# Weights split ahead at a closer pace, and attention's visits, early output tiles and item distance in another order, in a hybrid encoder step

## Chip, cores and metric

One core of a Trainium2 chip. The metric is the device time of one execution in microseconds (us); the time before is the median of 3 runs. PE is the matrix engine (PEld its weight loads), DVE, ACT and POOL are the vector, scalar and GpSimd engines, SP issues nearly all DMAs.

## Reference

A trunk of two layers over 1024 prompt frames and 32 sample frames, computed as one set of 1056 columns. Layer 0 has an mLSTM mixer, layer 1 a windowed attention with a sink per head and ALiBi; both have a SwiGLU FFN and a LayerNorm after each part.

```python
kv = (x @ w_kv).reshape(B, T, 2, N_KV_HEADS, HEAD_DIM)      # layer 1: two K/V heads, 64 wide
q = (x @ w_q).reshape(B, nc, CHUNK, N_KV_HEADS, GROUP, HEAD_DIM)     # 16 query heads, chunks of 64
s = jnp.einsum('bcqhgd,bckhd->bchgqk', q, k).astype(F32) * (HEAD_DIM ** -0.5) + bias
mx = jnp.maximum(jnp.max(s, -1, keepdims=True), sk)
p = jnp.exp(s - mx)
p = p / (jnp.sum(p, -1, keepdims=True) + jnp.exp(sk - mx))
mix = jnp.einsum('bchgqk,bckhd->bcqhgd', p.astype(v.dtype), v).reshape(B, T, D_ATT) @ w_out
x = layer_norm(DEEPNORM_ALPHA * x + mix, ln_g[layer, 0], ln_b[layer, 0])
x = layer_norm(DEEPNORM_ALPHA * x + swiglu(x, w_gu[layer], w_down[layer]), ln_g[layer, 1], ln_b[layer, 1])
```

## The kernel before

Activations lie transposed, model dimension on partitions: `act` (f32) and `sx`, its high and low half in fp32r. Every product of f32 values is three matmuls (L433 to L435): weight high by activation high, weight high by activation low, weight low by activation high. So each weight is split too: ACT casts the high half (L258, `wh`), and POOL or DVE subtracts (L260, `wl`). The class `Weights` walks a list of units (weight tiles of 128 x 1024) in the order in which PE will want them. It loads each raw (L172, `wr`, four buffers), splits it half by half into five slots, and takes the next as a slot falls free and 1.7 planned us have passed (`FEED_W`). Units in `W.ready` are not split there: their halves were stored in DRAM (`halves`) and are only loaded (L253).

**Order.** All engines run their instructions in the order in which the program emits them, and there is one emitting program. It emits dense matmuls (`gemm`), and after each k step it tells a `Weave` how long the three matmuls should take: 3 x (max(columns, 256) / 2400 + 0.003) planned us. The Weave then steps its side tasks, generators that emit a few instructions and yield a pause in planned us. So a pause says how much dense work is emitted until the task's next piece, not a time on the chip.

**`split_before`** is such a task. It starts in the first up tile of layer 0's FFN (in `summed`) and stores the halves of the 18 weights in `BEFORE` (wkv 0 and 1, wqb 0 to 7, wout_b 0 to 7): load `wraw` (L1318), pause; then for each half a cast on ACT into the one buffer `whi` (L1322), a pause of 1.5, a subtraction on DVE in place (L1324), a pause of 1.8, two stores (L1327), and a pause. There is one `wraw` and one `whi`, so the next cast waits for the store of the last. It is drained at the latest at the end of the down projection.

**The FFN** has, in each layer, 20 up tiles (`up_tile`) of seven products each, by a scheme of seven products for eight, with banks `A` and `B`; ACT copies bank A between products. Then come four down blocks of two tiles (`down`, here called down tiles, the seven products again), whose banks DVE adds into act (L1587, L1589). From the last up tile on, X is reloaded from DRAM (L1535) for the down tiles. Layer 1's FFN runs the same code without `split_before`.

**Attention** covers the 16 heads as 8 pairs j, two to a `jp`, and the columns as 9 blocks b of 128 (the ninth is the sample), three to a group g (384, 384 and 288 columns). A visit is one (jp, g): two query projections (`q_group`, 48 matmuls of the group's width) and six items (j, b). `JG` lists the visits: first (0,0) to (3,0), then for each jp group 1 and group 2. An item passes through scores (L1879, bank `psS`), exponential on ACT (L1900), scaling on POOL (L1913), transposes (L1938, bank `T`), halves (L1942, L1943), for each second item the values (L1967, one bank `O`) and `place`, which adds the result into act (L1981, L1985). The task `attention` runs these stages as a pipeline; `GAP_A` is its pause after a score and after a transpose, and twice that after values, 3 x GAP_A per item. The main loop emits the query projections of the next visit and first waits, emitting nothing dense, until the last visit but one has been scored.

**Output projection.** `out_tile` (L1270 adds its bank into act) multiplies one output tile of 128 rows with one quarter of 264 columns. The first three tiles of quarter 0 (`EARLY`) are emitted inside attention, in the visits (0,2), (1,2) and (2,2); the first of them drains attention until group 0 is placed, and the splitting of group 0. `mixed_parts` is a task that splits the placed attention output into sx (cast on ACT L463, low half L464) and reloads the residual into act (L1244, L1246, `scrx`). Quarter 0 reads `U_OUT_B[0]`, from stored halves; quarters 1 to 3 read `U_OUT_B[1]`, the same weights split again: the first two with POOL, the others with DVE.

Of the kernel before, what the change touches and what calls it, by code (L numbers as in the profile page):

```python
# [31 lines left out]
EARLY = 3  # L32
# [13 lines left out]
RAW = 4  # L46
SLOTS = 5
GAP_M = (0.6, 1.666, 1.519, 1.5)
GAP_A = 0.46

FEED_W = 1.7

# [18 lines left out]
CH = [(c, c * P, P if c < 8 else DEC, c // 3, (c % 3) * P) for c in range(9)]  # L71
# [233 lines left out]
def kernel(ctx: ExitStack, tc: tile.TileContext, A, O):  # L305
    nc = tc.nc
    ctx.enter_context(tc.manual_schedule())
    wv = Weave()
# [34 lines left out]
    for j in range(PAIRS):  # L343
        U_Q.append(add("wqk", 2 * j))
        U_K.append(add("wqk", 2 * j + 1))
        v = ("wv", 2 * j - 2) if j else ("wvg", 0)
# [21 lines left out]
    U_KV, U_QB, U_OUT_B = [], [[], []], [[], []]  # L368
# [2 lines left out]
        U_QB[0] += [add("wqb", u) for u in range(b, b + 4)]  # L371
    for jp in range(QH // 4):
        U_QB[1] += [add("wqb", 2 * jp + i) for i in range(2)]
        if jp < EARLY:
            U_OUT_B[0].append(add("wout_b", jp))
    U_OUT_B[0] += [add("wout_b", u) for u in range(EARLY, 8)]
    U_OUT_B[1] += [add("wout_b", u) for u in range(8)]
    add_ffn(1)
# [2 lines left out]
    on_vector.update((u, f) for u in U_Q[:1] for f in range(2))  # L381
    W = Weights(nc, base, units, pairs, on_vector, set())
    BEFORE = [("wkv", i) for i in range(2)] + [("wqb", i) for i in range(8)] + [("wout_b", i) for i in range(8)]
    for us in (*U_KV, *U_QB, U_OUT_B[0]):
        name = "wkv" if len(us) == 2 else "wqb" if us is not U_OUT_B[0] else "wout_b"
        W.ready.update((u, BEFORE.index((name, i))) for i, u in enumerate(us))
    W.early = {up[i] for up in U_UP for i in range(FIRST, FT)}
    wv.feed = W.feed

# [48 lines left out]
    def psbank():  # L438
        return new(psx[1][0], "d", [P, 512], F32, bufs=psx[1][1])
# [9 lines left out]
    def wcols(u):  # L449
        a, b = W.get(u)  # L450
        return tiles_of(a) + tiles_of(b)
# [10 lines left out]
    def split_act(k, g, low=nc.vector):  # L462
        nc.scalar.copy(sxh[k][g][:], act[k][g][:])  # L463
        low.tensor_sub(sxl[k][g][:], act[k][g][:], sxh[k][g][:].bitcast(F32))  # L464


    def group(g):
        return slice(g * N4, (g + 1) * N4)


    QUARTERS = [(group(g), (g % 2, slice(0, N4))) for g in range(4)]
# [606 lines left out]
    task = gtask = None  # L1078
# [153 lines left out]
    def mixed_parts(src, free, mixed, pauses, low=(nc.vector,), runs=WHOLE):  # L1232


        for (g, ks), pause in zip(runs, pauses):
            t0, n = GRP[g]
            while not free(g):
                yield 0.3
            for k in ks:
                while not mixed(k, g):  # L1240
                    yield 0.3
                split_act(k, g, low[k % len(low)])
                if g == 0:
                    nc.sync.dma_start(act[k][g], src[:, k, t0 : t0 + n])  # L1244
                elif k % 4 == 3:
                    nc.sync.dma_start(act_g[g][:, k - 3 : k + 1], src[:, k - 3 : k + 1, t0 : t0 + n])  # L1246
                yield pause
            if ks[-1] == KT - 1:
                nparts[0] += 1
# [15 lines left out]
    def out_tile(u, m, cols):  # L1265

        ps = psbank()[:, :N4]
        gemm(ps, wcols(u), [(SX[:, 0, k, cols], SX[:, 1, k, cols]) for k in range(KT)])
        z = ACT[:, m, cols]
        nc.vector.scalar_tensor_tensor(z, z, ALPHA, ps, op0=ALU.mult, op1=ALU.add)  # L1270
# [41 lines left out]
    def split_before():  # L1312

        ex = ExitStack()
        p = ex.enter_context(pool("before"))
        raw, hi = new(p, "wraw", [P, D]), new(p, "whi", [P, D // 2], F32R)
        for i, (name, idx) in enumerate(BEFORE):
            nc.sync.dma_start(raw[:], A[name][idx])  # L1318
            yield 9.0
            for f in range(2):  # L1320
                r = raw[:, f * (D // 2) : (f + 1) * (D // 2)]
                nc.scalar.copy(hi[:], r)  # L1322
                yield 1.5
                nc.vector.tensor_sub(r.bitcast(F32R), r, hi[:].bitcast(F32))  # L1324
                yield 1.8
                for k, t in enumerate((hi[:].bitcast(F32), r)):
                    nc.sync.dma_start(W.halves[:, i, f, k, :], t)  # L1327
                yield 2.0 if f else 4.5
            W.stored.add(i)
        ex.close()  # L1330

# [344 lines left out]
    n = D // 2  # L1676
# [164 lines left out]

    ast = {"ready": 0, "scored": 0, "placed": 0, "v": 0, "visit": -1}

    JG = [(jp, 0) for jp in range(4)] + [(jp, g) for jp in range(4) for g in (1, 2)]
    QG = [(2 * jp + i, g) for jp, g in JG for i in range(2)]

    def last_item(j, g):
        return 6 * JG.index((j // 2, g)) + 6

    def attention(gap):  # L1850
        S, pairs_ = {}, {}

        def parts(b):
# [115 lines left out]
        def place(j, b):  # L1969
# [12 lines left out]
            for h in range(2):  # L1982
# [4 lines left out]
        always = lambda j, b: True  # L1987
        yield 4.0
        yield from pipeline(
            [(2 * jp + i, 3 * g + b) for jp, g in JG for b in range(3) for i in range(2)],  # L1990
            [
                (scores, lambda j, b: ast["ready"] > QG.index((j, CH[b][3])), 0, (gap,) * 8),
                (soft, always, 0, 0),
                (scale, always, 0, 0),
                (turn, always, 2, (gap,) * 8),
                (values, lambda j, b: ast["v"] > b, 1, (0.0, 2 * gap) * 4),
                (place, always, 0, 0),
            ],
            (5, 3, 2, 1, 0, 4),
# [4 lines left out]
        wv.drain(t)  # L2004
    wv.launch(v_turn(0, 1.5))
    wv.launch(v_turn(1, 5.0))
    task = wv.launch(attention(GAP_A))
    ast["ready"] = 4
    keys_values(2)
    wv.launch(v_turn(2, 2.5))  # L2010
# [8 lines left out]
    def q_made():  # L2019
        yield 2.5  # L2020
        ast["ready"] += 1
# [6 lines left out]

    for n, (jp, g) in enumerate(JG):
        if n < 2:  # L2030
            continue
        while ast["scored"] < 6 * (n - 1):
            wv.tick(0.25)
        for j in (2 * jp, 2 * jp + 1):
            q_group(j, g)
            wv.launch(q_made())
            if g != 1:
                W.done(U_QB[g > 0][j])
        if n == 3:
            nparts[0] = 0  # L2040
            parts = wv.launch(
                mixed_parts(
                    scr,
                    lambda g: ast["ready"] > QG.index((7, g)),
                    lambda k, g: ast["placed"] >= last_item(k, g),
                    (2.4, 1.5, 1.5, 1.0, 1.0),
                    (nc.gpsimd,),
                    [WHOLE[0], *((g, ks) for ks in (range(6), range(6, KT)) for g in (1, 2))],
                )
            )  # L2050
        if g == 2 and jp < EARLY:
            before(0)
            out_tile(U_OUT_B[0][jp], jp, QUARTERS[0][0])
            W.done(U_OUT_B[0][jp])

    def finish():
        wv.drain(task)
# [137 lines left out]
```

## Time and profile before

| | us |
|---|---|
| median of 3 runs (all: 2201.12, 2201.32, 2202.99) | 2201.32 |
| the profiled execution, its own time | 2202.94 |
| its span, first to last instruction | 2201.2 |
| granted clock, mean | 0.995 |
| `split_before`, first load to last store (L1318, L1327) | 531.6 to 970.9 |
| stretch of layer 0's FFN (up and down) | 520.6 to 1104.7 |
| attention's score matmuls | 1216.6 to 1403.2 (first and last start) |
| stretch of layer 1's FFN | 1538.9 to 2111.7 |

All times of the trace are counted from the start of the span. A row of a group or a timeline names line, engine, operation and tiles as out<-in. In brackets stands how long the engine had been idle before it, and what ended that. A view of stretches has a row for each: its length, then each engine's busy time and number of instructions in the order PE, PEld, DVE, ACT, POOL, then granted clock (1.00 is full), DMA share and GB/s. Engine names with a q are instructions of the sequencer, such as DMA issues.

### The profile page before, as it was taken

Reading aid. Unit: us, or ns where it says so; the run is one execution under the profiler, and the core shown is the slowest. Engines: PE = TensorE matmul, PEld = TensorE weight load, DVE = VectorE, ACT = ScalarE, POOL = GpSimd, SP = SyncE. Lnnn points to the kernel's source line nnn. Section 1 sums busy time; section 2 is a strip of 40 time slices with the busy share of each in tenths; the row PEclk is TensorE's granted clock in tenths of the full one; section 3 lists DMA queues with packets and bytes.
Section 4 is the critical chain, followed back from the end, with each engine's and each line's share of the span. In section 5 each row is a group of like instructions: output and inputs, shape, how many; then the busy total and the mean of one; then the engine's idle time right before and its main releaser. Section 6 shows DMA issues by size and latency. Waiting matters only on the chain.

```text
span 2201.2 us, 44080 instructions
## 1 busy us (share of the span) xinstructions
PE 2166.9 (98%) x16982; PEld 2142.1 (97%) x16982; DVE 1469.2 (67%) x2822; ACT 995.0 (45%) x2243; POOL 917.1 (42%) x928
## 2 busy tenths in 40 slices
PE   9999999999999999989999999999999999999997
PEld 9999999999999999989999999999999999999997
DVE  4465676788777776556657776788666566466657
ACT  4443455465444444321235676656444444431125
POOL 2544310004666665444432443500665555554441
PEclk9999999999999999999999999999999999999999
DMA  5221212212665666797617542611344433497712
GB/s 171 77 63 57 58 40 87 89 39 86 216 220 204 226 207 208 267 329 263 190 52 234 163 126 85 223 49 39 128 147 157 147 138 147 137 350 249 251 53 80
DMA packets 191250, 332.99 MB, mean 151 GB/s; under 512 B 19200, under 2 KB 124728, under 8 KB 191040
## 3 DMA queue, kind: packets, MB, share of 16 engines
q1 hardware_dynamic: 186688, 325.84, 44.3%
q10 hardware_dynamic: 4352, 4.33, 0.6%
q8 instruction: 134, 2.20, 0.4%
q14 instruction: 76, 0.62, 0.1%
HBM read 226.47 MB, written 101.82 MB: 149 GB/s over the span
## 4 chain that ended last, share of the span: by engine, by line
PE 87%; DVE 5%; DMA 4%; ACT 3%; issue 1%; SPq 0%; POOL 0%; ACTq 0%; DVEq 0%; POOLq 0%
PE d L433 11%; PE d L435 10%; PE d L434 10%; PE A L433 9%; PE A L435 9%; PE A L434 9%; PE B L433 7%; PE B L434 7%; PE B L435 7%; PE O L1967 1%; DMA sx<-hs_t 1%; PE psS L1879 1%; PE T L1938 1%; ACT act L536 1%; PE T L986 1%
## 5 line engine op out<-in xcount | busy, mean ns | idle before, releaser
L260 POOL TENSOR_TENSOR wl_s<-wr,wh_s 128x512 fp32r<-128x512 f32 x224 | 309.9, 1394 | 250.9 <-ACT wh_s L258 194.8
L433 PE MATMUL d<-sx,wh 128*128 128x264 f32 (+2 forms) x1040 | 331.9, 319 | 0.0
L260 POOL TENSOR_TENSOR wl_a<-wr,wh_a 128x512 fp32r<-128x512 f32 x112 | 158.5, 1419 | 395.3 <-ACT wh_a L258 390.2
L435 PE MATMUL d<-sx,wl 128*128 128x264 f32 (+2 forms) x1040 | 316.5, 304 | 2.4 <-POOL wl L260 2.4
L434 PE MATMUL d<-sx,wh 128*128 128x264 f32 (+2 forms) x1040 | 316.0, 304 | 0.5 <-POOL sx L464 0.5
L433 PE MATMUL A<-sx,wh_s 128*128 128x264 f32 x896 | 255.7, 285 | 4.5 <-DVE act L1587 4.5
L434 PE MATMUL A<-sx,wh_s 128*128 128x264 f32 x896 | 255.2, 285 | 0.0
L435 PE MATMUL A<-sx,wl_s 128*128 128x264 f32 x896 | 255.0, 285 | 0.0
L258 ACT CAST wh_s<-wr 128x512 fp32r<-128x512 f32 x224 | 135.5, 617 | 193.5 <-DVE wr L201 99.2
L433 PEld LDWEIGHTS d<-sx,wh 128*128 128x128 f32 x1040 | 196.4, 189 | 3.1 <-ACT wh L258 0.2
L435 PEld LDWEIGHTS d<-sx,wl 128*128 128x128 f32 x1040 | 195.8, 188 | 3.2 <-POOL wl L260 2.9
L434 PEld LDWEIGHTS d<-sx,wh 128*128 128x128 f32 x1040 | 196.6, 189 | 1.8 <-POOL sx L464 0.7
L433 PE MATMUL d<-sx,ex 128*128 128x264 f32 x624 | 180.8, 290 | 0.1
L434 PE MATMUL d<-sx,ex 128*128 128x264 f32 x624 | 177.2, 284 | 0.0
L435 PE MATMUL d<-sx,ex 128*128 128x264 f32 x624 | 176.9, 284 | 0.0
L433 PEld LDWEIGHTS A<-sx,wh_s 128*128 128x128 f32 x896 | 169.6, 189 | 4.7 <-ACT wh_s L258 4.7
L435 PEld LDWEIGHTS A<-sx,wl_s 128*128 128x128 f32 x896 | 169.8, 190 | 0.0
L434 PEld LDWEIGHTS A<-sx,wh_s 128*128 128x128 f32 x896 | 169.6, 189 | 0.0
L1383 POOL TENSOR_TENSOR z<-z 128x528 fp32r<-128x528 f32 x76 | 104.8, 1380 | 116.7 <-ACT z L1382 101.4
L433 PE MATMUL A<-ex,wh_s 128*128 128x264 f32 x448 | 127.5, 285 | 0.0
L434 PE MATMUL A<-ex,wh_s 128*128 128x264 f32 x448 | 127.1, 284 | 0.0
L435 PE MATMUL A<-ex,wl_s 128*128 128x264 f32 x448 | 127.1, 284 | 0.0
(374 smaller groups left out, 7155.4 us busy)
## 6 DMA issues: line engine op xcount, KB each, us to landing
wr<-in_gu SPq DMA_DIRECT2D x92, 512.0 KB, 4.0
hs_x<-z SPq DMA_DIRECT2D x72, 528.0 KB, 3.0
hs_t<-z SPq DMA_DIRECT2D x64, 528.0 KB, 3.2
sx<-hs_x SPq DMA_DIRECT2D x112, 264.0 KB, 5.8
sx<-hs_t SPq DMA_DIRECT2D x64, 264.0 KB, 6.2
ex<-hs_t SPq DMA_DIRECT2D x64, 264.0 KB, 6.1
wr<-in_dn SPq DMA_DIRECT2D x32, 512.0 KB, 6.1
wh<-halves SPq DMA_DIRECT2D x46, 256.0 KB, 2.9
```

What stands on the lines that cost most here:

```text
L258: self.nc.scalar.copy(hi, r)
L260: eng.tensor_sub(lo, r, hi.bitcast(F32))
L433: nc.tensor.matmul(out, ah, bh, start=start and k == 0, stop=False, **kw)
L434: nc.tensor.matmul(out, ah, bl, start=False, stop=False, **kw)
L435: nc.tensor.matmul(out, al, bh, start=False, stop=stop and k == last, **kw)
L536: nc.scalar.activation(z, z, AF.Identity, scale=gk, bias=bk)
L986: nc.tensor.matmul(pc[:, : 2 * (DV + 1)], keys, vt[j][:, c], start=True, stop=True)
L1383: eng.tensor_sub(lo.bitcast(F32R), buf(s), hi)
L1879: nc.tensor.matmul(ps[:rows, at : at + nk], lhs, k[:, k0 : k0 + nk], start=i == 0, stop=i == 1)
L1938: nc.tensor.transpose(pt[:nk, t, :rows], p[:rows, at : at + nk], ident[:rows, :rows])
L1967: nc.tensor.matmul(out, v[:nk], x, start=i == 0, stop=i == len(todo) - 1)
```

## The change

It does six things, all in order and pace.

1. `split_before` pauses 7.0 instead of 9.0 after a load, 3.0 instead of 4.5 after a first half, 1.5 instead of 2.0 after a second half.
2. The first two weights of `U_OUT_B[1]` (quarters 1 to 3) are read from the stored halves too, instead of being loaded raw and split on ACT and POOL.
3. For jp 0 to 2 the visit of group 2 comes before that of group 1; jp 3 keeps its order. A weight of the query projection is released after the later of the two.
4. The early output tiles 0, 1 and 2 are emitted in the visits (1,2), (2,2) and (3,2), and the list of units has them one pair later.
5. The item distance is 0.40 in the first six visits and 0.46 from the seventh on, through a list that the pipeline reads.
6. In `mixed_parts` of attention the low halves of groups 1 and 2 alternate between DVE and POOL (group 0 stays on POOL), at pauses of 1.3 instead of 1.5.

```diff
-GAP_A = 0.46
+GAP_A = (0.40, 0.46)
...
-        if jp < EARLY:
-            U_OUT_B[0].append(add("wout_b", jp))
+        if 0 < jp <= EARLY:
+            U_OUT_B[0].append(add("wout_b", jp - 1))
...
-    for us in (*U_KV, *U_QB, U_OUT_B[0]):
-        name = "wkv" if len(us) == 2 else "wqb" if us is not U_OUT_B[0] else "wout_b"
-        W.ready.update((u, BEFORE.index((name, i))) for i, u in enumerate(us))
+    for name, us in (("wkv", U_KV), ("wqb", U_QB), ("wout_b", (U_OUT_B[0], U_OUT_B[1][:2]))):
+        for us in us:
+            W.ready.update((u, BEFORE.index((name, i))) for i, u in enumerate(us))
...
+            lows = low if g else low[-1:]
...
-                split_act(k, g, low[k % len(low)])
+                split_act(k, g, lows[k % len(lows)])
...
-            yield 9.0
+            yield 7.0
...
-                yield 2.0 if f else 4.5
+                yield 1.5 if f else 3.0
...
-    JG = [(jp, 0) for jp in range(4)] + [(jp, g) for jp in range(4) for g in (1, 2)]
+    JG = [(jp, 0) for jp in range(4)] + [(jp, g) for jp in range(4) for g in ((2, 1) if jp < 3 else (1, 2))]
...
+    gaps = [[0.0] * 8, [0.0] * 8]
+
+    def pace(gap):
+        gaps[0][:] = [gap] * 8
+        gaps[1][:] = [0.0, 2 * gap] * 4
...
-                (turn, always, 2, (gap,) * 8),
-                (values, lambda j, b: ast["v"] > b, 1, (0.0, 2 * gap) * 4),
+                (turn, always, 2, gaps[0]),
+                (values, lambda j, b: ast["v"] > b, 1, gaps[1]),
...
+        if n == 6:
+            pace(GAP_A[1])
...
-            if g != 1:
+            if g != (1 if jp == 3 else 2):
                 W.done(U_QB[g > 0][j])
...
-                    (2.4, 1.5, 1.5, 1.0, 1.0),
-                    (nc.gpsimd,),
+                    (2.4, 1.3, 1.3, 1.0, 1.0),
+                    (nc.vector, nc.gpsimd),
...
-        if g == 2 and jp < EARLY:
+        if g == 2 and jp:
             before(0)
-            out_tile(U_OUT_B[0][jp], jp, QUARTERS[0][0])
-            W.done(U_OUT_B[0][jp])
+            out_tile(U_OUT_B[0][jp - 1], jp - 1, QUARTERS[0][0])
+            W.done(U_OUT_B[0][jp - 1])
```

Three places where the order of instructions changes. The first is DVE in the first two down tiles of layer 0 (`act` is what the banks A and B are added into, `wr` are raw weights of the down projection, `wraw` and `whi` belong to `split_before`). Before:

```order
L197 TENSOR_TENSOR wr_11171<-wr_11171,wr_11173 128x512
L1324 TENSOR_TENSOR wraw_6663<-wraw_6663,whi_6664 128x512
L1587 SCALAR_TENSOR_TENSOR act<-act,A_11316 128x2x264
L1587 SCALAR_TENSOR_TENSOR act<-act,A_11335 128x2x264
L200 TENSOR_TENSOR wr_11173<-wr_11173 128x512
L201 TENSOR_TENSOR wr_11173<-wr_11173,wr_11171 128x512
L1587 SCALAR_TENSOR_TENSOR act<-act,A_11583 128x2x264
L1587 SCALAR_TENSOR_TENSOR act<-act,A_11601 128x2x264
L203 TENSOR_TENSOR wr_11171<-wr_11171,wr_11173 128x512
L1589 TENSOR_TENSOR act<-act,B_11620 128x2x264
L1589 TENSOR_TENSOR act<-act,B_11636 128x2x264
L1324 TENSOR_TENSOR wraw_6663<-wraw_6663,whi_6664 128x512
```

The same place after the change (line numbers are one higher there):

```order
L197 TENSOR_TENSOR wr_11189<-wr_11189,wr_11191 128x512
L1588 SCALAR_TENSOR_TENSOR act<-act,A_11330 128x2x264
L1588 SCALAR_TENSOR_TENSOR act<-act,A_11349 128x2x264
L200 TENSOR_TENSOR wr_11191<-wr_11191 128x512
L201 TENSOR_TENSOR wr_11191<-wr_11191,wr_11189 128x512
L1588 SCALAR_TENSOR_TENSOR act<-act,A_11590 128x2x264
L1588 SCALAR_TENSOR_TENSOR act<-act,A_11606 128x2x264
L203 TENSOR_TENSOR wr_11189<-wr_11189,wr_11191 128x512
L1590 TENSOR_TENSOR act<-act,B_11625 128x2x264
L1590 TENSOR_TENSOR act<-act,B_11641 128x2x264
L1588 SCALAR_TENSOR_TENSOR act<-act,A_11590 128x2x264
L1588 SCALAR_TENSOR_TENSOR act<-act,A_11606 128x2x264
```

The subtractions of `split_before` are gone from here; its last one now stands in the third up tile from the end, with its last casts on ACT and stores on SP.

The second is PE between the second query projection of the last visit ahead of the first early output tile, and that tile (`T` are transposes, `psS` scores, `O` values, `d` a dense bank). Before, behind the projection's last matmul and one product of values:

```order
L1938 MATMUL T_15605<-ident,s_15399 128x128 x3
L1879 MATMUL psS_14481<-KH_14096,Q_15270 128x192
L1879 MATMUL psS_14481<-KL_14098,Q_15270 128x192
L1879 MATMUL psS_14481<-KH_14096,Q_15270 128x192
L1879 MATMUL psS_14481<-KL_14098,Q_15270 128x192
L1938 MATMUL T_15625<-ident,s_15451 128x128 x3
L1879 MATMUL psS_14482<-KH_14096,Q_15390 128x192
L1879 MATMUL psS_14482<-KL_14098,Q_15390 128x192
L1879 MATMUL psS_14482<-KH_14096,Q_15390 128x192
L1879 MATMUL psS_14482<-KL_14098,Q_15390 128x192
L1967 MATMUL O_15643<-hi_15557,VR 128x256
L1967 MATMUL O_15643<-lo_15558,VR 128x256
```

After the change, from the last scores of the projection into the tile:

```order
L1886 MATMUL psS_14481<-KH_14096,Q_15527 128x192
L1886 MATMUL psS_14481<-KL_14098,Q_15527 128x192
L1886 MATMUL psS_14481<-KH_14096,Q_15527 128x192
L1886 MATMUL psS_14481<-KL_14098,Q_15527 128x192
L433 MATMUL d_15859<-sx,wh_0_15715 128x264
L434 MATMUL d_15859<-sx,wh_0_15715 128x264
L435 MATMUL d_15859<-sx,wl_0_15716 128x264
L1945 MATMUL T_15865<-ident,s_15668 128x128 x3
L433 MATMUL d_15859<-sx,wh_0_15715 128x264
L434 MATMUL d_15859<-sx,wh_0_15715 128x264
L435 MATMUL d_15859<-sx,wl_0_15716 128x264
```

Before, 33 matmuls of attention follow each other there with no dense one between; now dense matmuls of the tile lie between its steps.

The third is SP at the end of quarter 0 (`act<-scrx` are residual reloads of four k tiles, `halves` the stored weight halves, `in_wout_b` raw weights). Before:

```order
L172 DMA wr_17431<-in_wout_b 128x1024
L1246 DMA act<-scrx 128x4x288
L1246 DMA act<-scrx 128x4x384
L1246 DMA act<-scrx 128x4x288
L172 DMA wr_17570<-in_wout_b 128x1024
L172 DMA wr_17576<-in_wout_b 128x1024
```

After:

```order
L172 DMA wr_17445<-in_wout_b 128x1024
L1247 DMA act<-scrx 128x4x384
L253 DMA wh_0_17511<-halves 128x512
L253 DMA wl_0_17512<-halves 128x512
L1247 DMA act<-scrx 128x4x288
L253 DMA wh_1_17562<-halves 128x512
L253 DMA wl_1_17563<-halves 128x512
L172 DMA wr_17566<-in_wout_b 128x1024
```

The halves of the second weight of quarters 1 to 3 now stand behind the residual reloads, where the raw loads of later weights stood.

More of the change, by code (lines that the diff above doesn't have):

```diff
@@ L1848, in last_item, with attention @@
         return 6 * JG.index((j // 2, g)) + 6
-    def attention(gap):
+    gaps = [[0.0] * 8, [0.0] * 8]
+    def pace(gap):
+        gaps[0][:] = [gap] * 8
+        gaps[1][:] = [0.0, 2 * gap] * 4
+    def attention():
         S, pairs_ = {}, {}
@@ L1991, in attention @@
             [
-                (scores, lambda j, b: ast["ready"] > QG.index((j, CH[b][3])), 0, (gap,) * 8),
+                (scores, lambda j, b: ast["ready"] > QG.index((j, CH[b][3])), 0, gaps[0]),
                 (soft, always, 0, 0),
                 (scale, always, 0, 0),
-                (turn, always, 2, (gap,) * 8),
-                (values, lambda j, b: ast["v"] > b, 1, (0.0, 2 * gap) * 4),
+                (turn, always, 2, gaps[0]),
+                (values, lambda j, b: ast["v"] > b, 1, gaps[1]),
                 (place, always, 0, 0),
@@ L2006 @@
     wv.launch(v_turn(1, 5.0))
-    task = wv.launch(attention(GAP_A))
+    pace(GAP_A[0])
+    task = wv.launch(attention())
     ast["ready"] = 4
```

## The prediction

> **What bounds the kernel now.** I read the page first: one engine fills the span.
>
> ```profile
> PE 2166.9 (98%) x16982; PEld 2142.1 (97%) x16982; DVE 1469.2 (67%) x2822; ACT 995.0 (45%) x2243; POOL 917.1 (42%) x928
> ```
>
> PE is busy for 2166.9 of 2201.2 us, so the change, which leaves the matmuls as they are, can only win idle time of PE (34.3 us in all) and time that PE ran at a lower clock. Next I read whom PE waited for (columns: us in total, times, longest).
>
> ```profile
> PE A L433 <- DVE act L1587: 6.2, 3, 4.5
> PE B L433 <- DVE act L1589: 3.0, 1, 3.0
> PE O L1967 <- DVE act L1985: 2.8, 2, 2.1
> PE d L435 <- POOL wl L260: 2.4, 2, 1.7
> PE T L1938 <- DVE lo L1943: 1.0, 1, 1.0
> PE d L434 <- POOL sx L464: 0.5, 1, 0.5
> ```
>
> The first two rows are the down projection of an FFN: PE waits until DVE has added a bank to act. The next four are attention and the output projection behind it. The change touches both places. For the first one the kernel has its own control: layer 1's FFN does the same work as layer 0's, but without the splitting of later weights. I cut both into up tiles, the first two down tiles and the rest (stretch, its length, busy us and instructions of PE, PEld, DVE, ACT, POOL, granted clock, DMA share, GB/s).
>
> ```profile
> 520.60:928.60 408.00, 408.00 (x3362) 408.00 (x3362) 290.79 (x300) 189.18 (x338) 251.91 (x177) 1.00 0.61 212
> 928.60:954.50 25.90, 22.38 (x171) 21.96 (x169) 15.76 (x24) 7.82 (x14) 11.51 (x9) 0.93 0.99 340
> 954.50:982.00 27.50, 22.95 (x168) 22.80 (x169) 13.57 (x21) 4.46 (x8) 9.72 (x8) 0.88 1.07 384
> ...
> 1538.90:1946.90 408.00, 408.00 (x3362) 408.00 (x3362) 243.69 (x267) 173.44 (x305) 235.72 (x177) 1.00 0.43 151
> 1946.90:1968.60 21.70, 20.57 (x170) 20.36 (x169) 14.99 (x22) 6.68 (x12) 12.42 (x9) 1.00 1.07 382
> 1968.60:1989.00 20.40, 20.35 (x168) 20.38 (x169) 13.24 (x20) 4.25 (x7) 9.39 (x7) 1.00 1.08 372
> ```
>
> The up tiles take 408.00 us in both layers: there the splitting costs PE nothing. The first two down tiles take 25.90 + 27.50 = 53.4 us in layer 0 and 21.70 + 20.40 = 42.1 us in layer 1, and only layer 0 loses clock (0.93 and 0.88). The chain of waits says why (start, us, what):
>
> ```profile
> 961.62 7.13 DMA halves<-whi
> ...
> 968.83 0.63 ACT whi L1322
> ...
> 969.48 0.69 DVE wraw L1324
> 970.17 0.63 DVE act L1587
> ...
> 970.94 0.56 PE A L433
> ```
>
> ACT stood before its copy into whi until the store of the previous half had landed, DVE stood behind ACT, the add into act behind that, and PE behind the add.
>
> **The splitting at a closer pace: 11.3 us gained.** By the code's pauses a weight takes 9.0 + 2 x (1.5 + 1.8) + 4.5 + 2.0 = 22.1 planned us, 18 weights 397.8. What they took, and what ACT waited for at L1322:
>
> ```profile
> L1318 SPq DMA_DIRECT2D wraw<-in_wkv x2: 333/378/424, 531.6 to 558.3; - x2
> ...
> L1327 SPq DMA_DIRECT2D halves<-wraw x36: 319/332/1243, 547.8 to 970.9; - x36
> ...
> DMA to landing us min/median/max: 3.1/4.6/6.8
> ...
>   DMA halves<-whi: 28.4, 7
> ```
>
> The landing row is that of the stores, and the last row says that ACT stood 28.4 us in 7 times for them already. From 531.6 to 970.9 are 439.3 us, 1.104 of the plan. After the change a weight takes 7.0 + 6.6 + 3.0 + 1.5 = 18.1, all of them 325.8 planned, so 359.8 us: they end near 891, 37 us ahead of the down projection at 928.6. The order of DVE and ACT agrees: no split step is left among the down tiles. What remains there is what layer 1 has, whose first down tile still holds a wait of about 1.2 us. The gain is 53.4 - 42.1 = **11.3 us**, the clock included.
>
> The price is in the up tiles. The copy of a weight's second half now follows the first half's store by 3.0 x 1.104 = 3.3 us instead of 5.0, and that store lands in 4.6 (median) to 6.8 us: ACT, and DVE and the bank copies queued behind it, stand for 1.3 us as a rule and 3.5 at worst. SP, which must not reload wraw before the second half's stores have landed, stands for 4.6 - 1.7 = 2.9 us per weight instead of 2.4; queued behind it are the FFN's weight loads, fetched ahead into four buffers. What hides ACT's wait is the B product between two A products: 24 matmuls of 408.00 / 3362 = 0.121 us are 2.9 us, less a copy of 0.63 leaves 2.3. So the median wait costs nothing and the worst one 1.2 us; the bounds are 0 and 18 x 1.2 = 21.6 us, and I take 0, since the old pace, with waits of the same kind, cost 0.00 of 408.
>
> **The early output tile moved one visit later: 3.7 us.** Before, the first early tile asks for the last score block of the first four visits as soon as that visit's queries are emitted, so the rest of those blocks is emitted with no dense matmul between. PE and DVE there:
>
> ```profile
> 1283.56 0.27 PE L1879 MATMUL psS<-KL,Q 128*128 128x192 f32 x1
> 1285.89 0.36 PE L1967 MATMUL O<-hi,VR 128*128 128x256 f32 x1 [2.05 <-DVE act L1985]
> ...
> 1283.62 1.26 DVE L1740 SCALAR_TENSOR_TENSOR Q<-d,Q 64x256 fp32r<-64x256 f32 x4 [0.76 <-ACT Q L1737]
> 1284.89 0.85 DVE L1985 TENSOR_TENSOR act<-O,t 64x256 f32<-64x256 f32 x2
> 1285.77 0.56 DVE L1943 TENSOR_TENSOR lo<-T,hi 128x384 fp32r<-128x384 f32 x1
> ...
> 1272.00:1288.00 16.00, 13.67 (x100) 12.69 (x98) 13.07 (x58) 13.05 (x46) 7.59 (x11) 0.96 0.38 116
> 1288.00:1305.00 17.00, 17.00 (x123) 16.82 (x122) 10.69 (x42) 12.26 (x37) 7.54 (x10) 0.94 0.50 160
> ```
>
> Two value products follow each other across one bank, and the second waits 2.05 us for DVE, which had four query pieces ahead of the add. Behind it the granted clock is 0.96 over 16 us and 0.94 over 17 us, which costs 0.04 x 16 + 0.06 x 17 = 1.7 us. In the new order the tile stands one visit later, when those blocks are long placed, and dense matmuls lie between all of attention's steps. I take 2.05 + 1.7 = **3.7 us**; the bounds are 0 (an equal wait elsewhere) and 3.7. The Trainium skill ("TensorE: Matmul & The Clock Gate", Part 1) lets the clock fall only after an idle window of about 3.4 us; by that this wait would have kept its clock and the term would be 2.05, for a sum 1.7 lower. The trace does not agree: 0.96 and 0.94 stand behind a wait of 2.05 us.
>
> **Item distance and visit order: 0.4 us.** A visit of six items takes 6 x 3 x 0.40 = 7.2 planned us at first and 8.3 later, against the planner's dense 7.8 (two projections of 384 columns), 5.9 (288) or 8.6 (288 with an early tile). With 8.3 throughout, visits of 7.8 fell short and attention was emitted bare for a while; at 7.2 it runs ahead. The other wait for O, 2.8 - 2.05 = 0.75 us, came where two value products stood close behind a visit of 288 columns; I take half of it, 0.4, with bounds of -1.0 (one more such wait, as ACT and DVE get six items in less time) and 0.75. The wait of 1.0 us for T at attention's start stays, its surroundings being the same.
>
> **Two weights stored ahead, low halves on DVE too: 0.6 us.** At the start of the second quarter PE waited twice, 0.48 and 1.66 us:
>
> ```profile
> 1418.46 0.39 PE L434 MATMUL d<-sx,wh 128*128 128x264 f32 x1 [0.48 <-POOL sx L464]
> 1422.34 0.39 PE L435 MATMUL d<-sx,wl 128*128 128x264 f32 x1 [1.66 <-POOL wl L260]
> ...
> 1415.96 4.91 POOL L464 TENSOR_TENSOR sx<-act,sx 128x384 fp32r<-128x384 f32 x4 [0.25 <-ACT sx L463]
> ...
> wh<-halves SPq DMA_DIRECT2D x34, 256.0 KB, 2.9
> wl<-halves SPq DMA_DIRECT2D x34, 256.0 KB, 5.2
> ...
> act<-scrx SPq DMA_DIRECT2D x2, 768.0 KB
> ...
> act<-scrx SPq DMA_DIRECT2D x2, 576.0 KB
> ```
>
> POOL did four low halves in a row (4.91 us) and then the weight. Now eight of the sixteen low halves are DVE's, spread over the tiles before (a piece takes DVE between 0.56 us, its subtraction for lo of 384 above, and POOL's 4.91 / 4 = 1.2; I take 0.56 and nothing on the path, as PE asks for none of them until the quarter ends), and the two weights' four ACT copies, four POOL subtractions and two raw loads go: both waits, 2.1 us, end. What is late next is on SP: the second weight's halves are now issued behind residual loads of 768 and 576 KB, which wait for the last low halves. The last one is split about 1.5 us into the quarter (an estimate: two ACT casts and 1.2 of POOL behind the last placed item), so the pair goes out near 2.0, its low half lands 2.9 to 5.2 us later, at 5.3 to 7.6 with the issue between, and PE wants it 24 + 12 matmuls in, at 4.4 us. That is 0.9 to 3.2 us of a new wait; with 0 as the lower bound I take 1.5, nearer the row without other traffic (2.9). Net 2.1 - 1.5 = **0.6 us**, bounds -1.1 and 2.1. The Trainium skill ("DMA: Bandwidth & Descriptors", Queues, rings and completion order) has each DMA engine consume descriptors in ring order, so the pair would pass none of the residual's bytes and the upper price would hold, as in rival 1; no run here shows that queue by itself.
>
> **Sum.** 11.3 + 3.7 + 0.4 + 0.6 = 16.0 us. The profiled execution took 2202.94 us (span 2201.2 and 1.7 around it, taken as unchanged); less 16.0 that is 2186.9. The median of the runs is 2201.32, 1.6 lower, so I forecast 2185.3 us.
>
> **Rivals.** (1) *Attention gives nothing back*: the waits for O and T move to other visits, and the weight pair behind the residual waits the 3.2 us of its upper bound. For it: DVE is busy for 13.07 of 16 us around the wait at 1285.89, and a denser pace leaves it less room. Against it: dense work now lies between the steps. It gives 11.3 - 1.1 = 10.2, so 2191.1 us. (2) *The down tiles wait all the same*, for the reload of X, which moves 340 to 384 GB/s there in both layers; against it, layer 1 at 382 and 372 GB/s loses only 1.2 us. It gives 4.7, so 2196.6. (3) *Slower*: in the up tiles ACT's wait for the first half's store passes the 2.3 us that the B product hides, at each of 18 weights. From 16.0 / 18 = 0.9 us per weight on, the gain is gone; with the 1.2 of the worst store at every weight and half as much again for the clock, 18 x 1.8 = 32 us are lost, so 2217 us. Against it: the median store lands in time for PE, and the old pace lost nothing. (4) *The splitting doesn't end earlier*, because waits stretch each step: it has 37 us in hand, two per weight. It gives 4.7 as in (2).
>
> **How the numbers follow.** Forecast 0.69, (1) 0.21, (2) and (4) 0.06, (3) 0.04. Lower end: 11.3 and all of attention's waits (the last four rows of the second view, with 0.7 of the wl row in another stage, are 6.0, and 1.7 of clock) are 19.0, so 2182.3; less 1.3 for the runs' scatter (2201.12 to 2202.99), 2181. Upper end: (1), and 1.4 of scatter, 2192.5. Outside lie (2) to (4) and some of the edges, under 2 in 10. A measurement of this kernel tells about 0.2%, 4.4 us, from no change: (1) and the forecast are faster by more, (2) just so; 0.92 faster, 0.05 same, 0.03 slower.
>
> **What would show it.** Right: layer 0's first two down tiles near 42 us at clock 1.00 and no wait of ACT on halves among them; the up tiles still 408.0; no wait of 2 us for O and no clock below 0.99 near 1280; at the second quarter a wait on a DMA in the place of POOL. Wrong: up tiles above 409 with A waiting for ACT, or a sum of waits in attention above 6 us.

## The result, and the profile after the change

The changed kernel takes 2217.89 us (median of 5 runs, 2212.84 to 2223.25), the kernel before 2202.93 (5 runs, 2201.12 to 2204.15): a ratio of 1.0071, 95% interval 1.0051 to 1.0091, so 0.7% slower. The forecast was 2185.3 us with a range up to 2192.5. The profiled execution took 2221.01 us with a span of 2219.2, 18.0 more than before.

First the page's line of busy engines, after the change:

```profile
PE 2171.2 (98%) x16982; PEld 2142.1 (97%) x16982; DVE 1473.6 (66%) x2830; ACT 992.8 (45%) x2239; POOL 911.2 (41%) x916
```

PE is idle for 2219.2 - 2171.2 = 48.0 us in place of 34.3. Whom it waited for (us in total, times, longest), the first rows of the view of waits:

```profile
PE A L433 <- ACT z L1474: 8.1, 3, 3.9
PE A L433 <- ACT z L1467: 5.5, 2, 3.4
PE A L433 <- ACT z L1457: 3.2, 2, 3.0
PE A L433 <- DVE act L1588: 2.3, 2, 1.2
PE d L433 <- DMA wh<-halves: 2.1, 2, 1.1
...
PE A L435 <- POOL wl_s L260: 1.3, 1, 1.3
```

The first three rows are new: A of an *up* tile waits until ACT has copied the previous A out of its bank. The waits for DVE in the down tiles, which led the list before (6.2 and 3.0 us), have shrunk to 2.3. The same stretches as before, moved to where the tiles now lie (length, busy us and instructions of PE, PEld, DVE, ACT, POOL, granted clock, DMA share, GB/s):

```profile
521.90:956.90 435.00, 416.73 (x3363) 414.64 (x3363) 296.68 (x304) 189.29 (x341) 257.36 (x177) 0.98 0.59 206
956.90:979.30 22.40, 20.68 (x170) 20.29 (x168) 14.89 (x22) 6.68 (x12) 12.40 (x9) 1.00 1.07 378
979.30:999.70 20.40, 20.36 (x168) 20.39 (x169) 13.23 (x20) 4.25 (x7) 9.38 (x7) 1.00 1.08 372
1556.70:1964.80 408.10, 408.10 (x3363) 408.10 (x3362) 244.28 (x268) 173.56 (x305) 235.57 (x177) 1.00 0.42 151
```

Layer 0's up tiles, which were to stay at 408.0, take 435.0: 27.0 us lost, of which 435.00 - 416.73 = 18.3 are idle (16.8 of them in the three new rows) and 416.73 - 408.0 = 8.7 are clock (0.98 granted). Layer 1's up tiles, without splitting, still take 408.1. The first two down tiles take 22.4 + 20.4 = 42.8 us in place of 53.4: 10.6 gained. So layer 0's FFN alone accounts for 16.4 of the 18.0.

Why ACT is late stands in the view of split_before's copy into whi, before and after. Before, of the up tiles alone (560 to 925 us; the whole program had 28.4 in 7), and after, where all 36 casts fall among the up tiles:

```profile
  DMA halves<-whi: 10.8, 5
  DMA wraw<-in_wout_b: 5.0, 2
...
  DMA wraw<-in_wqb: 2.2, 1
```

```profile
  DMA halves<-whi: 67.0, 15
  issue: 12.1, 3
  DMA wraw<-in_wqb: 9.3, 4
  DMA wraw<-in_wout_b: 4.6, 4
  DMA wraw<-in_wkv: 4.4, 2
```

ACT now stands for the store of whi for 67.0 us in 15 times, a mean of 4.5, and for the load of wraw for 18.3 in 10. For the 12.1 us in 3 times (`issue`) the profile names no releaser; all three stand before a weight's first half, 4.3 to 5.5 us behind the issue of its load, so they are probably waits for the load too. One wait for the store from end to end, of the changed kernel: ACT's timeline, SP's, the chain of waits, and PE's timeline (start, us, what; in brackets the idle time before):

```profile
791.72 0.62 ACT L1323 CAST whi<-wraw 128x512 fp32r<-128x512 f32 x1 [0.93 <-DMA wraw<-in_wout_b]
...
793.79 0.62 ACT L258 CAST wh_a<-wr 128x512 fp32r<-128x512 f32 x1
801.73 0.62 ACT L1323 CAST whi<-wraw 128x512 fp32r<-128x512 f32 x1 [7.33 <-DMA halves<-whi]
...
802.77 0.59 ACT L1474 COPY z<-A 128x528 f32<-128x528 f32 x1
```

```profile
792.24 2.33 SPq L172 DMA_DIRECT2D wr<-in_gu  x2
794.80 0.33 SPq L1385 DMA_DIRECT2D hs_t<-z  x1
```

```profile
793.91 0.87 DVE z L1384
...
795.18 6.47 DMA halves<-whi
```

```profile
803.42 0.59 PE L433 MATMUL A<-sx,wh_s 128*128 128x264 f32 x1 [3.93 <-ACT z L1474]
```

ACT casts a weight's first half at 791.72, does four more instructions, and stands before the second half from 794.41 on. SP issues the store of the first half only at 795.18, behind two weight loads and a store of hs (`hs_t`), which itself went out only when DVE had finished its data at 794.78. The store of whi lands 6.47 us later; the copy of A stands behind the cast in ACT's queue, and PE waits 3.93 us for that bank. So ACT was at the next cast 0.77 us *before* the store went out, where the prediction had let 3.3 us pass behind it.

### The profile page after: what moved, and what is told of

It is laid out like the page before. It is cut to its first block, busy times and chain, and to the rows that moved or that the text cites. A ratio compares the mean times of both kernels' runs of the same rounds, so it can differ in the third digit from the quotient of the medians.

```text
span 2219.2 us, 44041 instructions
## 1 busy us (share of the span) xinstructions
PE 2171.2 (98%) x16982; PEld 2142.1 (97%) x16982; DVE 1473.6 (66%) x2830; ACT 992.8 (45%) x2239; POOL 911.2 (41%) x916
## 4 chain that ended last, share of the span: by engine, by line
PE 77%; DVE 7%; DMA 5%; ACT 4%; issue 4%; POOL 2%; SPq 0%; POOLq 0%; DVEq 0%; ACTq 0%
PE d L433 10%; PE d L435 10%; PE d L434 9%; PE A L433 8%; PE A L434 8%; PE A L435 8%; PE B L433 6%; PE B L434 6%; PE B L435 6%; DMA halves<-whi 1%; PE O L1974 1%; PE psS L1886 1%; POOL wl_s L260 1%; DMA hs_x<-z 1%; DMA sx<-hs_x 1%
```

## The experiments

The theory after the traces: at the closer pace ACT stands in line for split_before's DMAs among the up tiles, and PE waits for the bank copies behind it. Rivals: attention's part of the change does it, through the same planner; or the traffic of the splitting does it, wherever ACT stands.

**Which part of the change.** The changed kernel with the old pauses, and the kernel before with the new ones:

```diff
-            yield 7.0
+            yield 9.0
-                yield 1.5 if f else 3.0
+                yield 2.0 if f else 4.5
```

> The changed kernel with split_before's three pauses put back (9.0, 4.5, 2.0); attention's part of the change stays. Theory A (the closer pace costs the up tiles more than the down tiles gain; attention's part nets nothing): layer 0's FFN takes what it took before, up tiles near 408, first two down tiles near 26 and 27.5, and the time is 2217.9 - 16.5 = 2201.4, within 3 of the kernel before. Rival B (the order of attention's items, emitted by the same planner, or the two more weights stored ahead, disturbs the FFN): the up tiles still lose 20 us or more and the time stays near 2218. Rival C (the forecast's attention terms are real and are only masked): 2202.9 - 4.7 = 2198.

Measured: 2203.75 us, ratio to the kernel before 1.0006 (0.9997 to 1.0015).

```diff
-            yield 9.0
+            yield 7.0
-                yield 2.0 if f else 4.5
+                yield 1.5 if f else 3.0
```

> The kernel before with only split_before's pauses changed (7.0, 3.0, 1.5). Theory A: up tiles lose about 27 us in ACT waits for the store of whi, the first two down tiles gain 10, so 2202.9 + 16.5 = 2219. Rival B: the FFN gains 10 to 11 and loses nothing, 2192.

Measured: 2215.39 us, ratio 1.0058 (1.0041 to 1.0075). The pauses alone carry the loss, and without them there is none: rival B falls, and so does C, since 2198 lies below e1's interval.

**Which of the pauses.** On the kernel before, the pause between the halves alone, then the other two alone:

```diff
-                yield 2.0 if f else 4.5
+                yield 2.0 if f else 3.0
```

> The kernel before with only the pause between a weight's halves shortened, 4.5 to 3.0 (9.0 and 2.0 stay). Theory A in its narrow form (it is this pause, since the second half's cast overwrites whi while the first half's store is under way): the up tiles lose about 20 to 27 us; splitting ends 18 x 1.5 x 1.1 = 30 us earlier, near 941, so the down tiles gain some 7; in all 2202.9 + 13 to 20 = 2216 to 2223. Rival D (the shorter pause behind the load of wraw, or SP standing for it ahead of the FFN's own loads): no loss in the up tiles, 2202.9 - 7 = 2196.

Measured: 2208.33 us, ratio 1.0024 (1.0014 to 1.0034).

```diff
-            yield 9.0
+            yield 7.0
-                yield 2.0 if f else 4.5
+                yield 1.5 if f else 4.5
```

> The kernel before with only the other two pauses shortened, 9.0 to 7.0 and 2.0 to 1.5 (4.5 between the halves stays). Theory A in its narrow form: the up tiles lose nothing or little (below 5 us), splitting ends 18 x 2.5 x 1.1 = 50 us earlier, near 921 and ahead of the down projection, the down tiles gain 10: 2202.9 - 10 = 2193. Rival D: the up tiles lose as after the change and the time is near 2215.

Measured: 2210.14 us, ratio 1.0033 (1.002 to 1.0046). Both expectations failed. The pause between the halves costs the up tiles 9.0 us, not 20 to 27, and the other two cost them 16.5, not under 5. The stretch of the up tiles in e3 and in e4, and ACT's waits at the cast in e4:

```profile
521.00:938.00 417.00, 410.98 (x3363) 409.89 (x3362) 296.14 (x301) 187.93 (x339) 253.42 (x176) 1.00 0.59 208
```

```profile
520.80:945.30 424.50, 413.66 (x3362) 411.59 (x3361) 295.75 (x304) 189.91 (x341) 256.69 (x177) 0.99 0.61 211
```

```profile
  DMA halves<-whi: 33.9, 11
  DMA wraw<-in_wqb: 18.1, 6
  DMA wraw<-in_wkv: 5.7, 1
  DMA wraw<-in_wout_b: 4.7, 2
```

In e4, among the up tiles, the waits for the store are 33.9 us in place of 10.8, and those for the load are 28.5 in place of 7.2 (the rest of those before lay among the down tiles). PE's stalls stand behind both kinds; one behind a load, of e4:

```profile
589.53 0.62 ACT L1322 CAST whi<-wraw 128x512 fp32r<-128x512 f32 x1 [6.12 <-DMA wraw<-in_wqb]
...
592.25 0.39 PE L433 MATMUL A<-ex,wh_s 128*128 128x264 f32 x1 [2.17 <-ACT z L1456]
```

Four such stalls, 3.5 us in all, follow casts that had waited for a load, and three, 4.8 us in all, casts that had waited for a store (2.71, 0.36 and, by way of DVE's subtraction and the splits behind it, 1.75). The theory in its narrow form, this one pause and its store alone, falls; what is left is a wider one: any DMA of the splitting for which ACT stands. The two parts add up to 9.0 + 16.5 = 25.5; both together cost the up tiles 22.6 on the kernel before (e2) and 27.0 in the changed kernel.

**Where ACT stands, or the traffic.** Two kernels at the new pace in all, with the same bytes. In the first, whi is stored before VectorE's subtraction instead of behind it:

```diff
                 yield 1.5
+                nc.sync.dma_start(W.halves[:, i, f, 0, :], hi[:].bitcast(F32))
                 nc.vector.tensor_sub(r.bitcast(F32R), r, hi[:].bitcast(F32))
                 yield 1.8
-                for k, t in enumerate((hi[:].bitcast(F32), r)):
-                    nc.sync.dma_start(W.halves[:, i, f, k, :], t)
+                nc.sync.dma_start(W.halves[:, i, f, 1, :], r)
```

> The changed kernel, at its own pace, with the store of whi issued right behind the cast and ahead of VectorE's subtraction, so 1.8 planned us earlier. Theory A, widened after the runs on single pauses (whatever makes ACT stand in its own queue for a DMA of the splitting, store or load, delays the copies of A and B out of their banks, and PE waits for these): the waits for the store fall from 67 us in 15 to about 35, those for the load of wraw stay near 18; the up tiles lose 10 to 15 us in place of 27, and the time is 2217.9 - 12 to 17 = 2201 to 2206. Rival E (the loss comes with the traffic or the number of splitting steps per time, not with the place where ACT stands): nothing changes, 2218.

Measured: 2202.16 us, ratio 0.9997 (0.9988 to 1.0005). In the second, wraw is two tiles of half a weight in the same space, each loaded a step ahead, and both halves get the same pause:

```diff
+        load(0)
+        yield 7.0
+        for h in range(2 * len(BEFORE)):
+            i, f = divmod(h, 2)
+            r = raws[f][:]
+            if h + 1 < 2 * len(BEFORE):
+                load(h + 1)
+            nc.scalar.copy(hi[:], r)
+            yield 1.5
+            nc.sync.dma_start(W.halves[:, i, f, 0, :], hi[:].bitcast(F32))
+            nc.vector.tensor_sub(r.bitcast(F32R), r, hi[:].bitcast(F32))
+            yield 1.8
+            nc.sync.dma_start(W.halves[:, i, f, 1, :], r)
+            yield 5.75
```

> The changed kernel at the same pace in all (18.1 planned us a weight), but wraw is two buffers of half a weight, each loaded a whole step ahead, the two halves stand evenly (5.75 behind each), and whi's store goes out ahead of the subtraction. Theory A: neither the store (7.5 planned us to land in place of 3.0) nor the load (9 in place of 7, with no store to stand for) is late; the sum of ACT's waits for the splitting's DMAs falls from 85 us to under 15, the up tiles lose 0 to 3 us and the first two down tiles keep their gain of 10: 2202.9 - 7 to 11 = 2192 to 2196. Rival E: the same work at the same pace costs the same, 2213 to 2218.

Measured: 2192.34 us, ratio 0.9952 (0.994 to 0.9965). Of e6, in three views: the up tiles; all that ACT still waits for DMAs at its cast; the landing of whi's store:

```profile
520.60:928.70 408.10, 408.10 (x3362) 408.08 (x3361) 285.50 (x304) 191.07 (x341) 247.46 (x177) 1.00 0.64 220
```

```profile
  DMA halves<-whi: 9.9, 6
```

```profile
DMA to landing us min/median/max: 3.6/4.6/5.5
```

The up tiles lose nothing although they move 220 GB/s in place of 206, and the store takes 4.6 us to land in the median, as the stores did before the change. So it is not the traffic (rival E): it is that ACT arrives too early for the store or the load. How much of e6's gain the earlier loads give, and how much the even spacing, was not run apart; the earlier store alone is e5. The kernels side by side, from these views (us; the down column is layer 0's first two down tiles; the waits are ACT's at the cast, among the up tiles alone; the last of them those for which the profile names no DMA):

| kernel | up tiles | down | for the store (times) | for the load (times) | other (times) | time |
|---|---|---|---|---|---|---|
| before | 408.0 | 53.4 | 10.8 (5) | 7.2 (3) | 6.2 (2) | 2202.9 |
| after | 435.0 | 42.8 | 67.0 (15) | 18.3 (10) | 12.1 (3) | 2217.9 |
| e1, after with the old pauses | 408.1 | 53.0 | 18.3 (9) | 8.3 (3) | none | 2203.8 |
| e2, before with the new pauses | 430.6 | 41.7 | 66.6 (16) | 15.2 (9) | 12.5 (3) | 2215.4 |
| e3, before, pause between halves | 417.0 | 49.9 | 45.2 (12) | 4.6 (4) | none | 2208.3 |
| e4, before, other two pauses | 424.5 | 43.2 | 33.9 (11) | 28.5 (9) | 3.6 (1) | 2210.1 |
| e5, after, earlier store | 417.6 | 41.9 | 25.9 (12) | 22.2 (8) | 9.1 (3) | 2202.2 |
| e6, after, even halves | 408.1 | 41.8 | 9.9 (6) | none | 1.5 (1) | 2192.3 |

The loss goes with the sum of these waits. Where they sum to 11.4 us (e6), 24.2 (before) or 26.6 (e1) the up tiles lose at most 0.1; from there the loss rises in the order of the sums: 9.0 at 49.8 (e3), 9.6 at 57.2 (e5), 16.5 at 66.0 (e4), 22.6 at 94.3 (e2) and 27.0 at 97.4 (after). The length of a single wait does not set it. Two waits of the changed kernel, and PE behind the second:

```profile
677.19 0.62 ACT L1323 CAST whi<-wraw 128x512 fp32r<-128x512 f32 x1 [6.51 <-DMA halves<-whi]
...
615.97 0.62 ACT L1323 CAST whi<-wraw 128x512 fp32r<-128x512 f32 x1 [4.58 <-DMA halves<-whi]
...
617.66 0.39 PE L433 MATMUL A<-ex,wh_s 128*128 128x264 f32 x1 [3.02 <-ACT z L1457]
```

The wait of 6.51 us cost PE nothing: it ended while PE was still filling bank A, before a copy was due. The one of 4.58 lay across the moment at which a copy was due, and PE stood for 3.02. So between 1.6 us (4.58 - 3.02) and all of 6.51 was hidden, by where in the up tile the wait fell.

**Attention's parts, each alone on the kernel before.** First the order (visits, early output tiles, item distance), its diff cut to the core:

```diff
-GAP_A = 0.46
+GAP_A = (0.40, 0.46)
...
-    JG = [(jp, 0) for jp in range(4)] + [(jp, g) for jp in range(4) for g in (1, 2)]
+    JG = [(jp, 0) for jp in range(4)] + [(jp, g) for jp in range(4) for g in ((2, 1) if jp < 3 else (1, 2))]
...
-            out_tile(U_OUT_B[0][jp], jp, QUARTERS[0][0])
+            out_tile(U_OUT_B[0][jp - 1], jp - 1, QUARTERS[0][0])
```

> The kernel before with only the order in attention changed: the visits, the early output tiles one visit later, the item distance of 0.40 and 0.46. By the prediction's terms 3.7 + 0.4 = 4.1 us faster: 2198.8. By the trace after the change (the waits for O and T move to other visits, and none of the time comes back): 2202.9 within 1.5. It may even lose, if the denser items are what stretched the second quarter's start.

Measured: 2201.88 us, ratio 0.9997 (0.9988 to 1.0006): no difference. PE's waits between 1200 and 1410 us in e7:

```profile
PE O L1973 <- DVE act L1991: 1.4, 3, 0.5
PE T L1944 <- DVE st L1916: 1.3, 1, 1.3
PE O L1973 <- DVE lo L1949: 0.7, 1, 0.7
PE O L1973 <- ACT hi L1948: 0.6, 2, 0.4
PE psS L1885 <- DVE st L1891: 0.3, 1, 0.3
```

The wait of 2.1 us is gone, and the same time stands in several of at most 0.7 and a longer one for T: 1.4 + 1.3 + 0.7 + 0.6 + 0.3 = 4.3, against 2.8 for O, 1.0 for T and 0.2 for psS before. Then the other part, the two more weights stored ahead and the low halves:

```diff
-    for us in (*U_KV, *U_QB, U_OUT_B[0]):
...
+    for name, us in (("wkv", U_KV), ("wqb", U_QB), ("wout_b", (U_OUT_B[0], U_OUT_B[1][:2]))):
...
+            lows = low if g else low[-1:]
...
-                    (2.4, 1.5, 1.5, 1.0, 1.0),
-                    (nc.gpsimd,),
+                    (2.4, 1.3, 1.3, 1.0, 1.0),
+                    (nc.vector, nc.gpsimd),
```

> The kernel before with only the two more weights stored ahead and the low halves on VectorE too. By the prediction 0.6 us faster (2.1 of waits for POOL out, 1.5 of a new wait for a DMA in), 2202.3. By the trace after the change, where two waits for wh of 0.93 and 1.15 stand at that place: 0.0, 2202.9. Rival: the pair's wait behind the residual's loads costs more than the POOL waits gave back, 2204 or above.

Measured: 2206.96 us, ratio 1.0022 (1.0013 to 1.0031), slower by 4.1, as the rival had it. SP's queue, PE's wait, and the stretch behind it in e8:

```profile
1418.15 2.57 SPq L1247 DMA_DIRECT2D act<-scrx  x2
1420.82 0.46 SPq L253 DMA_DIRECT2D wh<-halves  x1
...
1425.11 0.59 PE L433 MATMUL d<-sx,wh 128*128 128x264 f32 x1 [3.29 <-DMA wh<-halves]
```

```profile
1424.00:1432.00 8.00, 6.76 (x32) 6.46 (x33) 3.08 (x6) 1.76 (x3) 0.00 (x0) 0.57 0.83 313
```

The weight's halves are issued behind both residual loads and land 4.3 us after that. PE waits 3.29 us in place of 0.48 + 1.66, 1.15 more, and the clock of 0.57 over 8 us costs 0.43 x 8 = 3.4; the two are about the loss.

**The second quarter's start, and what is best.** On e6, the residual's loads from POOL's queue, whose low halves they wait for:

```diff
-                    nc.sync.dma_start(act_g[g][:, k - 3 : k + 1], src[:, k - 3 : k + 1, t0 : t0 + n])
+                    q = nc.gpsimd if src is scr else nc.sync
+                    q.dma_start(act_g[g][:, k - 3 : k + 1], src[:, k - 3 : k + 1, t0 : t0 + n])
```

> The kernel with even halves, and the residual's loads for the second quarter (act from the scratch) issued by POOL's queue in place of SP's. Theory F (the pair of stored weights stands on SP behind the residual loads, which wait for the last low halves): the two waits for wh at the second quarter's start, 1.02 and 0.84 us, go, and the time is 2192.3 - 1.9 = 2190.4. Rival G (the weights' transfer itself is late, or POOL, which now issues loads, is what the low halves wait for next): 2192 or above, with a wait for a DMA or for POOL at the same place.

Measured: 2189.24 us, ratio 0.9935 (0.9923 to 0.9948), 3.1 below e6. PE's waits at the place (1395 to 1415 us), in e6 and in e9:

```profile
PE d L433 <- DMA wh<-halves: 1.9, 2, 1.0
```

```profile
PE d L435 <- DMA wl<-halves: 0.3, 1, 0.3
```

SP's queue was the cause of these waits (theory F); rival G falls. They account for 1.6 of the 3.1 us; the rest no row shows, and e6 was measured in an earlier session than e9, e10 and e11 (the kernel before took 2202.86 us there and 2203.11 here). Next the even halves on the kernel before, with nothing of attention's part:

> The kernel before with only the splitting in even halves at the closer pace in all; nothing of the change to attention. If attention's part of the change nets nothing: the first two down tiles give 53.3 - 42 = 11.3 and the up tiles lose nothing, 2202.9 - 11.3 = 2191.6, within 1 of the changed kernel with even halves (2192.3). If attention's part holds the 4.7 us of the prediction: 4.7 slower than that, 2197.

Measured: 2190.83 us, ratio 0.9943 (0.9931 to 0.9956). And e6 without the stored part (so order and splitting alone):

> The changed kernel with even halves and without the two more weights stored ahead and the low halves on VectorE: order and splitting alone. By the two parts' runs on the kernel before (order 2201.9, stored 2207.0, before 2202.9) the stored part costs and the order gives about 1: 2191.6 - 1 = 2190.6. If the stored part gives 0.6 as in the prediction: 2193.

Measured: 2190.46 us, ratio 0.9941 (0.9927 to 0.9954). Attention's part as a whole gives nothing: e6, which has it, lies 1.5 us above e10, and e11, without the stored weights, 0.4 below e10, with intervals that overlap. The best of all is e9, 0.65% below the kernel before and 1.3% below the changed one (2189.24 against 2217.89); its lead over e10 and e11, 1.2 to 1.6 us, is within the intervals, while the wait that it removes is seen in the rows.

## Why the prediction was wrong

**The step that failed** is the price in the up tiles: "the median wait costs nothing and the worst one 1.2 us; the bounds are 0 and 18 x 1.2 = 21.6 us, and I take 0, since the old pace, with waits of the same kind, cost 0.00 of 408". It was 27.0, above even its bound, with the very sign that the prediction had named for being wrong: up tiles above 409 with A waiting for ACT. Three things were wrong in it.

- *The distance from store to cast.* It was taken as 3.0 planned us, stretched, counted from the store's issue. A pause fixes only which instructions stand between on each engine. In the wait shown above ACT, busy for 45% of the span, ran through its four in 2.1 us, while SP issued the store late, behind its own loads and the store of hs: ACT arrived 0.77 us before the issue, so the wait was 7.33 us, not 3.5 at worst. E5, which does nothing but issue that store earlier, took back 17.4 of the 27.0.
- *The load was not priced.* For the shorter pause behind it only SP's standing was counted, 2.9 us for 2.4. In e4 ACT's waits for the load among the up tiles rose from 7.2 to 28.5 us, and stalls of PE stand behind them. The waits for the store rose there too, from 10.8 to 33.9, and how the 16.5 us that the up tiles lost divide between the two is not shown.
- *The clock was left out of the bound*: 8.7 of the 27.0.

That "waits of the same kind" had cost nothing was true, and the wrong thing to go by: those for the store among the up tiles were 10.8 us in 5 times, 2.2 each, and fell where PE did not need ACT. The cover of 2.3 us was near the tight case (1.6 was hidden at 615.97, where two casts stood between the wait and the copy); elsewhere up to 6.51 was hidden. What failed was the length and number of the waits set against it. The rival on record that ended slower, (3), had the place and the mechanism, at a chance of 0.04. That its 2217 us lie so near the 2217.9 is partly luck: it holds 32 us of loss in the up tiles, where 27.0 came, and 4.7 us of gain in attention that did not come, and its 1.8 us at each of 18 weights came in fact as seven stalls (the three new rows of PE's waits).

**Down tiles: right.** 11.3 was forecast, 10.6 came after the change and 11.6 in e6. The last store was issued later than forecast, since the waits stretched the steps (907.7 against 891; row below, of the changed kernel), but still ahead of the down projection at 956.9.

```profile
L1328 SPq DMA_DIRECT2D halves<-wraw x36: 319/427/2193, 546.4 to 907.7; - x36
```

**Early output tile and item distance, 3.7 + 0.4: wrong in size.** E7 shows 1.0 us, within its uncertainty of zero. The wait of 2.05 went as forecast; waits of the same sum came elsewhere, the lower bound that the prediction had named and not taken. The 1.7 us of clock come behind this wait in some executions only. In e10, whose attention is that of the kernel before and has the same wait of 2.1, the clock behind it is 1.00 (e10's waits between 1200 and 1395 us, and two of its stretches, which answer to those at 1272 and 1288 before):

```profile
PE O L1977 <- DVE act L1995: 2.8, 2, 2.1
```

```profile
1260.00:1276.00 16.00, 13.65 (x105) 12.66 (x104) 13.06 (x57) 13.35 (x49) 7.43 (x11) 1.00 0.39 117
1276.00:1293.00 17.00, 17.00 (x130) 16.75 (x129) 11.83 (x46) 12.90 (x40) 8.82 (x12) 1.00 0.51 160
```

Of the six profiled executions with this attention and this wait (2.05 to 2.07 us), the clock fell in four (before, e2, e3 and e8, to between 0.93 and 0.97 in these stretches) and stayed at 1.00 in two (e4 and e10). In e7 it stayed at 1.00 throughout attention, so its 1.0 us may be this clock; that lies within its uncertainty.

**Stored weights, 0.6: the mechanism was right, the size wrong.** The new wait stands where it was forecast, behind the residual's loads on SP, and e9 shows that SP's queue makes it (in the kernel with even halves). Alone it was 3.29 us (0.9 to 3.2 was the range, 1.5 taken), and the clock behind it was not in the price; the bounds of -1.1 to 2.1 did not hold the -4.1 of e8. With the new order it is 2.1 us after the change, which is what the two POOL waits had been.

By the measured terms: 10.6 - 27.0 = -16.4 for the FFN, about 0 for attention, and 1.6 us of the 18.0 outside these stretches.

## What to carry to other kernels

A pause in a planner's schedule is an order of instructions, not a time: before a step that reuses a buffer is moved closer to the DMA that must free it, read in the trace when the waiting engine would arrive and when the queue would issue that DMA. Price such waits by their sum over the stage and by what stands behind the waiting instruction in its engine's queue when PE needs it, here the copies that free PE's banks. If the pace must rise, spread the distances first: the same pace with even steps, loads a step ahead and stores issued at once turned 0.7% slower into 0.5% faster, in the same space.

## What the runs showed of the hardware

How far a wait of PE costs clock changes from one wait to another. In the changed kernel's up tiles the clock fell behind waits of 3.36, 3.02, 3.93 and 3.56 us and not behind those of 1.27 and 2.16. Stretches of 3.4 us behind a wait of 3.36, one of 2.16 and one of 3.93:

```profile
577.90:581.30 3.40, 3.36 (x15) 3.36 (x16) 1.17 (x2) 1.67 (x3) 3.09 (x3) 0.50 0.66 265
...
793.40:796.80 3.40, 3.40 (x28) 3.40 (x29) 2.85 (x3) 1.00 (x2) 2.26 (x2) 1.00 0.77 188
803.40:806.80 3.40, 3.38 (x16) 3.38 (x17) 3.29 (x3) 1.24 (x3) 3.40 (x3) 0.53 0.01 5
```

Behind one and the same wait of 2.1 us in attention it fell in four of six executions, as told above. The Trainium skill ("TensorE: Matmul & The Clock Gate", Part 1) calls the window of about 3.4 us free-running, and the warm-up run-variable for that reason; that the fall of the clock varies between executions here goes with a free-running window, though no run shows the window itself. By its table the clock falls after at least one idle window; the drop behind 3.02 us, and that behind 2.05 before, show that an idle time shorter than the window can be enough.
